# Hybrid encoder step on one core: the mixers' stores and the gate preparation's transfers issued from GpSimd instead of SyncE

## The chip, the cores and the metric

The kernel runs on one core of one Trainium2 chip. The metric is device time in microseconds (us), the median of several executions; less is better. The engines are called TensorE (PE in the profile), VectorE (DVE), ScalarE (ACT), GpSimd (POOL) and SyncE (SP). PE multiplies matrices, DVE, ACT and POOL work on elements, and SP computes nothing: it issues DMA transfers, in the order of its own program. ACT and POOL can issue DMAs too, each in its own order.

## The reference

One layer of an encoder works on two groups that share weights: a prompt of 2048 tokens, and 8 streams with 16 new tokens each. Width 1024, feed-forward 2816.

```python
h = rms_norm(x, norm_g[0])
z = h @ w_in
qa, ka, va, qb, kb, vb, ob, ib, fb = jnp.split(z, IN_SPLITS, axis=-1)
att = band_attention_prompt(...)  # streams: band_attention_step
att = rms_norm(att, g_att)
hb, (c1, n1, m1) = mlstm_sequence(qh, kh, vh, ig, lf, c0, n0, m0)
hb = hb * lax.rsqrt(jnp.mean(hb * hb, axis=-1, keepdims=True) + EPS)
mlstm_out = (hb * g_mlstm * jax.nn.sigmoid(ob)).astype(x.dtype)
mix = jnp.concatenate([att, mlstm_out], axis=-1) @ w_out
x = x + rms_norm(mix, norm_g[1])
ffn, new_buf = conv_ffn(rms_norm(x, norm_g[2]), conv_buf, w_up, w_conv, b_conv, w_down)
x = x + rms_norm(ffn, norm_g[3])
```

The attention has 8 heads of 64, each over its chunk and the 8 chunks before it. The second mixer, an mLSTM, has 4 heads of 128 with a matrix state `c` per head, a normaliser `n` and a running maximum `m`; its gates `ig` and `lf` weigh products of queries and keys by exponentials of cumulative sums. All is float32. The new keys and values, `c`, `n`, `m` and the last rows of the convolution are outputs too.

## The kernel before, in words

The tokens stand in 17 tiles of 128 rows, 16 of the prompt (`SEQ`) and one of the streams (`SAMPLE`). A float32 product is made as three products of two rounded pieces: `mm3` (L95, L96, L97) issues them, so nearly all of PE's rows carry these lines. Casts and subtractions on ACT and DVE make the pieces (`qs`, `kh`, `skh` and so on).

**Stages.** Until about 1066 us the kernel runs through two halves of the tokens with 14 column groups of `w_in` each (names `va`, `qk`, `qb`, `vo`; results `qk_st` and so on are copied out of PE's memory at L224 and L226 and stored by ACT's DMAs at L239). Between these products a planner (`pump`) lays pieces of two streams of work, the attention (`heads`) and the mLSTM (`mems`). Then comes the output projection (`project`, rows of `wo`, until about 1340 us), and then the feed-forward blocks, which the change doesn't touch.

**Data through device memory.** Much is stored to device memory by one step and read back in another layout by a later one:

- `load_head` (L325 to L351) loads `nb` (a band of the relative bias, from `relrow`), `qraw`, `kraw` and `vraw` of an attention head out of `qTd`, `kTd`, `vd`. POOL then clears two corners of `nb` (L326, L327). L440 stores the head pair's result `attst` to `mixd`.
- `prep_sample` (L600 to L626) and `prep_prompt` (L553 to L585) prepare the gates. They store rows `md` and `dd` to device memory, and read `dd` back at once as `dec`, spread over 128 partitions. `mlstm` loads `mb` from `md` (L664), and POOL masks it (L673).
- `finish_heads` (L640 to L655) ends a pair of mLSTM tiles: `ad` and `mf` on POOL, `num` on DVE, then the store of `num` to `mixd` (or `mixs` for the streams).
- `mlstm_sample` goes through the 8 streams' states in four steps `bp` of two: load `cs` (L769), `qz` on POOL (L771, L774), products `cus` on PE (L781, L782), the new `cs` on DVE, its store to `c_sample` (L787). `cs` has two buffers.
- `attention_sample` loads cached keys `skr` and values `svr` of a stream (L847, L897), POOL copies the new columns into `skr` (L848), ACT casts to `skh` (L852), and L911 stores the result to `atts`.
- `project` loads the mixers' rows `mr` back, multiplies, normalises with a root that POOL makes (L78, L84, `n_rs`, `att_rs`), adds the input `xr` on POOL (L1027) and stores the tile to `x2d` (L1028). `mx` and `xr` share one buffer of two, which the load of L1004 fills again.

**What sets the order.** The kernel is built with a scheduler that simulates its own timeline and writes each engine's order from it; buffers come free when their last reader, a DMA included, is done. Each DMA also gets a completion lane. SP and ACT share eight of them in turn, and an issue waits until the transfer that last had its lane has landed; transfers of POOL have eight lanes of their own. An engine that waits, for data, a buffer or a lane, holds all that stands behind it in its order.

Of the kernel before, what the change touches and what calls it, by code (L numbers as in the profile page):

```python
# [17 lines left out]
P = 128  # L18
# [3 lines left out]
DB = 8  # L22
DS = 16
HA = 8
DA = 64
HB = 4
DH = 128
# [17 lines left out]
def hymba_step(ctx: ExitStack, tc: tile.TileContext, I: dict, O: dict):  # L45
    nc = tc.nc
# [317 lines left out]
    def att_unit(s, g2, j):  # L364
# [68 lines left out]
        for jj in range(4):  # L433
# [3 lines left out]
            st.rearrange("p a (h d) -> p a h d", h=2),  # L437
            ao.rearrange("p (a h d) -> p a h d", a=4, h=2),
            rinv.unsqueeze(3).broadcast_to([P, 4, 2, DA]), op=ALU.mult)
        nc.sync.dma_start(mixd[kg][:, :, pair * P:(pair + 1) * P], st)  # L440
        yield 0.43, 0.7

    def att_stream():
# [103 lines left out]
    def prep_prompt(half):  # L547
        n = 8
        ig, lf, nlf = log_gates(1 + 8 * half, n, f"p{half}")
        f2 = lambda t: t.rearrange("p c h -> p (c h)")  # L550
        yield 0.3, 0.8
        a, b = cum_rows(f2(ig), f2(lf), f2(nlf), 32, tri, f"p{half}")
        ca = pm.tile([P, P], F32, tag="kw", name=f"cm{half}", bufs=2)[:32, :]  # L553
        nc.vector.tensor_tensor_scan(ca, a, a, NEG, op0=ALU.max, op1=ALU.max)
        yield 0.3, 0.4
        rt = ps_sm(f"rt{half}")
        transpose(rt[0:1, 0:32], ca[:, P - 1:P], 32)
        transpose(rt[0:1, 32:64], b[:, P - 1:P], 32)
        row = pm.tile([1, 2, n, HB], F32, tag="rowl", name=f"rowl{half}", bufs=1)
        nc.vector.tensor_copy(row.rearrange("p a c h -> p (a c h)"), rt[0:1, 0:64])  # L560
        o = 8 * half
        for h in range(HB):
            nc.vector.tensor_tensor_scan(mrow[:, o + 1:o + 9, h], row[:, 0, :, h], row[:, 1, :, h],
                                         mrow[:, o:o + 1, h], op0=ALU.max, op1=ALU.add)
        yield 0.3, 0.5
        mp = ps_sm(f"mp{half}")
        transpose(mp[0:32, 0:1], mrow[:, o:o + 8, :].rearrange("p c h -> p (c h)"), 1)
        mprev = small.tile([32, 1], F32, tag="mprev", name=f"mprev{half}")
        nc.vector.tensor_copy(mprev, mp[0:32, 0:1])
        yield 0.3, 0.8  # L570
        pk = pm.tile([P, P], F32, tag="kw", name=f"pk{half}", bufs=2)
        nc.vector.tensor_scalar(ca, ca, mprev, None, op0=ALU.max)
        nml = small.tile([32, 1], F32, tag="nml", name=f"nml{half}")
        nc.vector.tensor_scalar(nml, ca[:, P - 1:P], -1.0, None, op0=ALU.mult)
        nc.vector.tensor_copy(pk[0:32, :], a)
        nc.scalar.activation(pk[32:64, :], ca, AF.Exp, bias=mprev, scale=-1.0)
        nc.vector.tensor_tensor(b, b, ca, op=ALU.add)
        nc.scalar.activation(pk[64:96, :], b, AF.Exp, scale=-1.0)
        nc.scalar.activation(pk[96:128, :], a, AF.Exp, bias=nml)
        md = dt_([32, P], f"md{half}")  # L580
        dd = dt_([32, 1], f"dd{half}")
        nc.sync.dma_start(md, ca)
        nc.sync.dma_start(dd, pk[32:64, P - 1:P])
        dec = pm.tile([P, n, HB], F32, tag="dec", name=f"dec{half}", bufs=1)
        nc.sync.dma_start(dec, dd.rearrange("(c h) o -> o c h", c=n).broadcast_to([P, n, HB]))  # L585
        yield 0.0, 0.8
        cols = pack_columns(pk, "p")
        stab[half] = (md, dec, cols)
        yield 0.3, 0.8

    def prep_sample():
        ig, lf, nlf = log_gates(0, 1, "s")
        trib = pm.tile([P, P], F32, tag="wexp", name="trib", bufs=2)
        nc.gpsimd.affine_select(out=trib, in_=tri, pattern=[[-DS, DB], [0, DS]], compare_op=ALU.is_ge, fill=0.0,
                                base=0, channel_multiplier=1)
        reset = pm.tile([P, P], F32, tag="kw", name="reset", bufs=2)[:HB, :]
        nc.gpsimd.memset(reset, 0.0)
        nc.gpsimd.memset(reset.rearrange("p (b s) -> p b s", b=DB)[:, :, 0:1], NEG)
        f2 = lambda t: t.rearrange("p c h -> p (c h)")
        a, b = cum_rows(f2(ig), f2(lf), f2(nlf), HB, trib, "s")  # L600
        yield 0.3, 0.8
        ms = small.tile([HB, DB], F32, tag="mss", name="mss")
        nc.sync.dma_start(ms, I["state_m"])
        ca = pm.tile([P, P], F32, tag="kw", name="cms", bufs=2)[:HB, :]
        nc.vector.tensor_tensor_scan(ca, reset, a, 0.0, op0=ALU.add, op1=ALU.max)
        v3 = lambda t: t.rearrange("p (b s) -> p b s", b=DB)
        msb = ms.unsqueeze(2).broadcast_to([HB, DB, DS])
        nc.vector.tensor_tensor(v3(ca), v3(ca), msb, op=ALU.max)
        mn_ = small.tile([HB, DB], F32, tag="mnew", name="mnew")
        nc.vector.tensor_tensor(mn_, v3(ca)[:, :, DS - 1], v3(b)[:, :, DS - 1], op=ALU.add)  # L610
        nc.sync.dma_start(O["m_sample"], mn_)
        pk = pm.tile([P, P], F32, tag="kw", name="pks", bufs=2)
        nc.vector.memset(pk, 0.0)
        nc.vector.tensor_copy(pk[0:HB, :], a)
        nc.vector.tensor_tensor(v3(pk[32:32 + HB, :]), msb, v3(ca), op=ALU.subtract)
        nc.vector.scalar_tensor_tensor(pk[64:64 + HB, :], b, -1.0, ca, op0=ALU.mult, op1=ALU.subtract)
        nc.vector.tensor_tensor(v3(pk[96:96 + HB, :]), v3(a), v3(ca)[:, :, DS - 1:DS].broadcast_to([HB, DB, DS]),
                                op=ALU.subtract)
        for o in (32, 64, 96):
            nc.scalar.activation(pk[o:o + HB, :], pk[o:o + HB, :], AF.Exp)  # L620
        md = dt_([HB, P], "mds")
        dd = dt_([HB, DB], "dds")
        nc.sync.dma_start(md, ca)
        nc.sync.dma_start(dd, v3(pk[32:32 + HB, :])[:, :, DS - 1])
        dec = pm.tile([P, HB, DB], F32, tag="decs", name="decs", bufs=1)
        nc.sync.dma_start(dec, dd.unsqueeze(0).broadcast_to([P, HB, DB]))  # L626
        yield 0.0, 0.8
        cols = pack_columns(pk, "s")
        stab["s"] = (md, dec, cols)
        yield 0.3, 0.8  # L630


    def finish_heads(num, enm, og, h, nch, dst, name):

        den = num[:, :, 0]
        ad = small.tile([P, 2], F32, tag="ad", name=f"ad{name}")[:, :nch]
        ssq = small.tile([P, 2], F32, tag="mssq", name=f"mssq{name}")[:, :nch]
        nc.vector.scalar_tensor_tensor(ad, den, -1.0, den, op0=ALU.mult, op1=ALU.max)
        nc.vector.tensor_tensor(ad, ad, enm, op=ALU.max)
        for c in range(nch):  # L640
            jk = pm.tile([P, P], F32, tag="wexp", name=f"jk{name}_{c}", bufs=2)
            nc.scalar.activation(jk, num[:, c, 1:DH + 1], AF.Square, accum_out=ssq[:, c:c + 1])
        nc.vector.tensor_tensor(ad, ad, ad, op=ALU.mult)
        nc.vector.scalar_tensor_tensor(ad, ad, DH * EPS, ssq, op0=ALU.mult, op1=ALU.add)
        f = small.tile([P, 2], F32, tag="mf", name=f"mf{name}")[:, :nch]
        nc.gpsimd.tensor_scalar(ad, ad, 1.0 / DH, 0.0, op0=ALU.mult, op1=ALU.add)
        nc.gpsimd.tensor_tensor(f, ad, nhalf[:, :nch], op=ALU.pow)
        nc.scalar.activation(og, og, AF.Tanh, scale=0.5)
        nc.vector.scalar_tensor_tensor(og, og, 1.0,
                                       hgm[h].unsqueeze(1).broadcast_to([P, nch, DH]),  # L650
                                       op0=ALU.add, op1=ALU.mult)
        for c in range(nch):
            nc.vector.scalar_tensor_tensor(num[:, c, 1:DH + 1], num[:, c, 1:DH + 1], f[:, c:c + 1], og[:, c, :],
                                           op0=ALU.mult, op1=ALU.mult)
        nc.sync.dma_start(dst, num[:, :, 1:DH + 1])  # L655

    def mlstm(h, half):
        md, dec, cols = stab[half]
# [21 lines left out]
        def chunk(s, c):  # L680
# [29 lines left out]
            finish_heads(num, cols[:, 2, r0:r0 + HB + 1:HB], s.og, h, 2,  # L710
                         mixd[sg][:, o:o + 2, 512 + h * DH:512 + (h + 1) * DH], s.nm)
            if half == 1 and s.pc == 3:
                nc.sync.dma_start(O["c_prompt"][h], cst[h])
            yield 0.0, 1.3

        pairs = [SimpleNamespace(pc=pc, t0=8 * half + 2 * pc, nm=f"{h}_{8 * half + 2 * pc}") for pc in range(4)]
# [9 lines left out]
    def mlstm_sample(h):  # L726
# [38 lines left out]
        def batches(bp):  # L765
# [18 lines left out]
                                           op0=ALU.mult, op1=ALU.add)  # L784
            nc.vector.tensor_tensor(cs, cs, dec[:, h, bs].unsqueeze(2).broadcast_to([P, 2, e]), op=ALU.mult)
            nc.vector.tensor_tensor(cs, cs, cu[:, :2 * e].rearrange("p (b e) -> p b e", b=2), op=ALU.add)
            nc.sync.dma_start(O["c_sample"][h][:, bs], cs)  # L787
            yield 0.85, 0.8

        def finish():  # L790
# [28 lines left out]
    def attention_sample(b0, b1):  # L819
# [74 lines left out]
        def values(b, kk):  # L894
# [13 lines left out]
            if kk == 4:  # L908
                so = pa.tile([P, 512], F32, tag="attT", name=f"so{b}", bufs=1)
                nc.vector.tensor_scalar(so, s.ot, s.rs, None, op0=ALU.mult)  # L910
                nc.sync.dma_start(atts[b], so)  # L911
            yield 0.64, 0.1

        yield queries()
# [47 lines left out]
    def project(tiles):  # L962
# [34 lines left out]
        for n_, s in enumerate(ss):  # L997
# [27 lines left out]
            rs = rsqrt_mean(ssq, D, f"n1_{t}", ssa)  # L1025
            nc.vector.scalar_tensor_tensor(m, m, rs, g1[0], op0=ALU.mult, op1=ALU.mult)
            nc.gpsimd.tensor_tensor(xr, m, xr, op=ALU.add)  # L1027
            nc.sync.dma_start(x2d[t], xr)  # L1028

# [224 lines left out]
                mems.append(lambda i=i: mlstm_sample(i))  # L1256
    for cost in out:
        pump(*cost)
    nc.sync.dma_start(O["m_prompt"], mrow[:, 16, :])


    p3, halo = ffn.p3, ffn.halo
# [431 lines left out]
```

## Time and profile before

| | |
|---|---|
| median of 3 executions | 2796.95 us (2793.69 to 2801.31) |
| the profiled execution, its own time | 2796.47 us |
| its span in the profile | 2794.8 us |
| mean granted clock of TensorE | 0.996 |
| PE, DVE, ACT, POOL busy | 2729.5, 1877.1, 1407.9, 429.6 us |
| moved to and from device memory | 486.05 MB, 174 GB/s in the mean |

The queues of DMAs in use were SP's, with 274590 packets and 449.21 MB, and ACT's, with 38592 packets and 33.83 MB; two queues of instructions carry the remaining 3 MB. POOL issued none.

Reading the rows: in a table of waits stand the engine and line that waited, what ended the wait, then microseconds in total, how often, and the longest. "SPq" is SP's queue of DMA issues, "ACTq" that of ACT. A timeline row has its start and duration in us, engine, line, operation, output and input, and in brackets the idle time just before it with what ended it. A row by stretch of time has for each engine busy us and the number of instructions, then TensorE's granted clock, the share of the DMA engines that was busy, and GB/s. A group's row ends with shortest, median and longest nanoseconds, or for a DMA with the median us from issue to landing.

### The profile page before, as it was taken

Reading aid. Unit: us, or ns where it says so; the run is one execution under the profiler, and the core shown is the slowest. Engines: PE = TensorE matmul, PEld = TensorE weight load, DVE = VectorE, ACT = ScalarE, POOL = GpSimd, SP = SyncE. Lnnn points to the kernel's source line nnn. Section 1 sums busy time; section 2 is a strip of 40 time slices with the busy share of each in tenths; the row PEclk is TensorE's granted clock in tenths of the full one; section 3 lists DMA queues with packets and bytes.
Section 4 is the critical chain, followed back from the end, with each engine's and each line's share of the span. In section 5 each row is a group of like instructions: output and inputs, shape, how many; then the busy total and the mean of one; then the engine's idle time right before and its main releaser. Section 6 shows DMA issues by size and latency. Waiting matters only on the chain.

```text
span 2794.8 us, 47058 instructions
## 1 busy us (share of the span) xinstructions
PE 2729.5 (98%) x16587; PEld 2554.0 (91%) x16587; DVE 1877.1 (67%) x3442; ACT 1407.9 (50%) x2836; POOL 429.6 (15%) x876
## 2 busy tenths in 40 slices
PE   8899999999999999999999999999999999999998
PEld 7899999998899998888999988899999878999887
DVE  5244455655556668766999986457777864888855
ACT  4354555534356666534545555345455543555543
POOL 1000010211100002344211110011111210222221
PEclk9999999999999999999999999999999999999999
DMA  5534355557555456346655555644444774555685
GB/s 187 150 117 137 105 169 162 164 151 212 160 174 149 140 170 185 114 157 220 199 175 167 169 177 174 220 142 153 160 154 140 275 267 151 172 177 177 195 299 192
DMA packets 313419, 486.05 MB, mean 174 GB/s; under 512 B 55426, under 2 KB 150622, under 8 KB 313054
## 3 DMA queue, kind: packets, MB, share of 16 engines
q1 hardware_dynamic: 274590, 449.21, 50.7%
q10 hardware_dynamic: 38592, 33.83, 3.6%
q8 instruction: 130, 2.13, 0.3%
q14 instruction: 107, 0.88, 0.1%
HBM read 359.36 MB, written 126.70 MB: 174 GB/s over the span
## 4 chain that ended last, share of the span: by engine, by line
PE 55%; DVE 2%; DMA 1%; issue 1%; POOL 1%; ACT 1%; SPq 0%; DVEq 0%; POOLq 0%; ACTq 0%
PE uec L95 6%; PE uec L96 6%; PE uec L97 6%; PE dn L97 4%; PE dn L96 4%; PE dn L95 4%; PE ua L97 3%; PE ua L96 3%; PE ua L95 3%; PE dnm L97 2%; PE dnm L95 2%; PE dnm L96 2%; PE wo L97 2%; PE wo L95 2%; PE wo L96 2%; PE ub L96 1%
## 5 line engine op out<-in xcount | busy, mean ns | idle before, releaser
L95 PE MATMUL uec<-B,wuh 128*128 128x384 f32 (+1 forms) x720 | 234.9, 328 | 0.9 <-DVE uu L1418 0.7
L96 PE MATMUL uec<-B,wuh 128*128 128x384 f32 (+1 forms) x720 | 235.2, 327 | 0.0
L97 PE MATMUL uec<-B,wul 128*128 128x384 f32 (+1 forms) x720 | 234.0, 327 | 0.0
L1266 DVE TENSOR_TENSOR gl<-gr,gh 128x768 fp32r<-128x768 f32 (+3 forms) x141 | 121.7, 872 | 154.1 <-ACT gh L1265 145.7
L1265 ACT CAST gh<-gr 128x768 fp32r<-128x768 f32 (+3 forms) x141 | 102.0, 736 | 200.1 <-PE dn L96 184.3
L1265 ACT CAST wuh<-wu 128x512 fp32r<-128x512 f32 x255 | 141.7, 618 | 113.0 <-PE uec L96 100.9
L95 PE MATMUL dn<-wdh,gh 128*128 128x512 f32 x466 | 182.9, 393 | 2.2 <-DVE ug L1418 2.2
L96 PE MATMUL dn<-wdl,gh 128*128 128x512 f32 x466 | 184.1, 395 | 0.0
L97 PE MATMUL dn<-wdh,gl 128*128 128x512 f32 x466 | 168.3, 396 | 0.0
L1266 DVE TENSOR_TENSOR wul<-wu,wuh 128x512 fp32r<-128x512 f32 x255 | 164.7, 684 | 2.8 <-DMA x2d<-mx 2.8
L393 DVE CUSTOM_DVE_ANT_0 tmp<-s,nb 128x640 f32<-128x640 f32 (+4 forms) x128 | 94.4, 737 | 92.5 <-PE s L383 91.1
L95 PE MATMUL vo<-wi_h,hT 128*128 128x256 f32 x544 | 155.9, 287 | 0.6 <-DVE mt L199 0.6
L97 PE MATMUL vo<-wi_h,hT 128*128 128x256 f32 x544 | 156.4, 288 | 0.0
L96 PE MATMUL vo<-wi_l,hT 128*128 128x256 f32 x544 | 155.6, 286 | 0.0
L95 PE MATMUL qk<-hT,wi_h 128*128 128x384 f32 (+1 forms) x384 | 129.8, 338 | 8.7 <-ACT qk_st L224 7.7
L95 PEld LDWEIGHTS uec<-B,wuh 128*128 128x128 f32 x720 | 135.1, 188 | 2.7 <-DVE uu L1418 1.2
L96 PEld LDWEIGHTS uec<-B,wuh 128*128 128x128 f32 x720 | 135.4, 188 | 0.2
L97 PEld LDWEIGHTS uec<-B,wul 128*128 128x128 f32 x720 | 135.2, 188 | 0.0
L406 DVE TENSOR_TENSOR ptl<-pt,pth 128x640 fp32r<-128x640 f32 (+4 forms) x128 | 93.6, 737 | 54.9 <-ACT pth L405 53.7
L394 ACT ACTIVATE tmp<-tmp,mn 128x640 f32<-128x640 f32 (+4 forms) x128 | 97.6, 762 | 64.5 <-DVE mn L393 62.1
L96 PE MATMUL qk<-hT,wi_h 128*128 128x384 f32 (+1 forms) x384 | 129.1, 336 | 0.0
L97 PE MATMUL qk<-hT,wi_l 128*128 128x384 f32 (+1 forms) x384 | 128.7, 335 | 0.0
(411 smaller groups left out, 8876.7 us busy)
## 6 DMA issues: line engine op xcount, KB each, us to landing
wu<-in_w_up SPq DMA_DIRECT2D x220, 256.0 KB, 4.0
wu<-wsd SPq DMA_DIRECT2D x176, 256.0 KB, 4.8
wdr<-in_w_down SPq DMA_DIRECT2D x132, 256.0 KB, 5.1
gr<-gd SPq DMA_DIRECT2D x78, 384.0 KB, 4.2
wi_raw<-in_w_in SPq DMA_DIRECT2D x52, 512.0 KB, 3.9
wsd<-ws SPq DMA_DIRECT2D x88, 256.0 KB, 2.7
gd<-g SPq DMA_DIRECT2D x44, 384.0 KB, 3.5
kraw<-kTd SPq DMA_DIRECT2D x112, 128.0 KB, 3.4
```

What stands on the lines that cost most here:

```text
L95: nc.tensor.matmul(out, ah, bh, start=start, stop=False, skip_group_check=onto)
L96: nc.tensor.matmul(out, ah, bl, start=False, stop=False, skip_group_check=onto)
L97: nc.tensor.matmul(out, al, bh, start=False, stop=stop, skip_group_check=onto)
L393: nc.vector.tensor_tensor_reduce(o_, s_, b_, 1.0, 3e38, ALU.add, ALU.min, accum_out=mn)
L394: nc.scalar.activation(tmp[:, :n], tmp[:, :n], AF.Exp, bias=mn, scale=-1.0, accum_out=rsum[:, i % 4, hh:hh + 1])
L406: nc.vector.tensor_tensor(s.ptl[:, sl, qc], ptv, s.pth[:, sl, qc], op=ALU.subtract)
L1265: nc.scalar.copy(h, r)
L1266: nc.vector.tensor_tensor(l, r, h, op=ALU.subtract)
```

## The change

At 15 places the call of a DMA moves from SP to POOL. In all 109 transfers move. Data, sizes and destinations stay as they are.

```diff
-        nc.sync.dma_start(mixd[kg][:, :, pair * P:(pair + 1) * P], st)
+        nc.gpsimd.dma_start(mixd[kg][:, :, pair * P:(pair + 1) * P], st)
...
-        nc.sync.dma_start(md, ca)
-        nc.sync.dma_start(dd, pk[32:64, P - 1:P])
+        nc.gpsimd.dma_start(md, ca)
+        nc.gpsimd.dma_start(dd, pk[32:64, P - 1:P])
         dec = pm.tile([P, n, HB], F32, tag="dec", name=f"dec{half}", bufs=1)
-        nc.sync.dma_start(dec, dd.rearrange("(c h) o -> o c h", c=n).broadcast_to([P, n, HB]))
+        nc.gpsimd.dma_start(dec, dd.rearrange("(c h) o -> o c h", c=n).broadcast_to([P, n, HB]))
...
-        nc.sync.dma_start(dst, num[:, :, 1:DH + 1])
+        nc.gpsimd.dma_start(dst, num[:, :, 1:DH + 1])
...
-            nc.sync.dma_start(O["c_sample"][h][:, bs], cs)
+            nc.gpsimd.dma_start(O["c_sample"][h][:, bs], cs)
...
-                nc.sync.dma_start(atts[b], so)
+                nc.gpsimd.dma_start(atts[b], so)
...
-            nc.sync.dma_start(x2d[t], xr)
+            nc.gpsimd.dma_start(x2d[t], xr)
```

These are L440 (16 transfers), L582, L583 and L585 (two each), L655 (36), L787 (16), L911 (8) and L1028 (17). The same is done with the load of `ms` (L603), the stores of `m_sample` (L611), `mds` and `dds` (L623, L624), the load of `decs` (L626), the four stores of `c_prompt` (L713) and that of `m_prompt` (L1259). Further back, in the feed-forward blocks, SP goes on issuing stores too (`wsd`, `gd`, `f0d`, the outputs).

Since the scheduler orders every engine anew, rows move that the diff doesn't name. ACT in the first column group, where `qk_st` of the first `qk` group is copied out and `qs` of the first attention head is cast from the loaded `qraw`:

```order
 L224 COPY qk_0_st_0_1068<-qk_0_1_0_1000 128x384
 L239 DMA kTd_0_78<-qk_0_st_0_1068 128x384
-L342 CAST qs_0_1290<-qraw_0_1263 128x512
 L224 COPY qk_0_st_1_1110<-qk_0_1_1_1071 128x384
 L239 DMA kTd_0_78<-qk_0_st_1_1110 128x128
 L239 DMA kTd_1_79<-qk_0_st_1_1110 128x256
+L342 CAST qs_0_1290<-qraw_0_1263 128x512
 L1175 CAST wi_h_1165<-wi_raw_1180 128x512 x2
```

The cast now comes behind the copy of `qk_st` and its stores. SP a little later in the same stretch, from the load of a `w_in` piece on, where `prep_prompt` had its transfers:

```order
 L1169 DMA wi_raw_1245<-in_w_in 128x1024
 L337 DMA kraw_0_0_1335<-kTd_0_78 64x512 x2
-L582 DMA md_1136<-cm_1065 32x128
-L583 DMA dd_1137<-pk_1127 32x1
 L351 DMA vraw_0_0_1367<-vd_0_114 128x4x64
-L585 DMA dec_1140<-dd_1137 128x32
-L302 DMA relrow<-ext 128x767 x2
+L334 DMA qraw_1_1484<-qTd_1_95 64x512 x2
 L1169 DMA wi_raw_1446<-in_w_in 128x1024
-L334 DMA qraw_1_1484<-qTd_1_95 64x512 x2
```

`md`, `dd` and `dec` are gone from SP, and the last two broadcasts of `relrow` (which now stand ahead of the first `qraw`) no longer precede the `wi_raw` load. The third place is the second half's `prep_prompt`, beside the cached keys of stream 6. On SP before:

```order
L847 DMA skr6_0_9190<-in_cache_k 128x512
L847 DMA skr6_1_9219<-in_cache_k 128x512
L582 DMA md1_8472<-cm1_8367 32x128
L583 DMA dd1_8473<-pk1_8463 32x1
L664 DMA mb0_8_10342<-md1_8472 128x2x128
L585 DMA dec1_8476<-dd1_8473 128x32
L847 DMA skr6_2_9248<-in_cache_k 128x512
L847 DMA skr6_3_9280<-in_cache_k 128x512
```

On POOL now, while SP issues the four `skr6` loads in a row:

```order
L848 COPY skr6_0_9190<-own4_8631 128x16
L848 COPY skr6_1_9219<-own4_8631 128x16
L582 DMA md1_8472<-cm1_8367 32x128
L848 COPY skr6_2_9248<-own4_8631 128x16
L583 DMA dd1_8473<-pk1_8463 32x1
L848 COPY skr6_3_9280<-own4_8631 128x16
L585 DMA dec1_8476<-dd1_8473 128x32
L673 AFFINE_SELECT mb0_8_10342<-mb0_8_10342 128x256
```

The preparation's three transfers have changed queue: they stood between two pairs of loads, and stand now between POOL's copies into the same buffers.

More of the change, by code (lines that the diff above doesn't have):

```diff
@@ L602, in prep_sample @@
         ms = small.tile([HB, DB], F32, tag="mss", name="mss")
-        nc.sync.dma_start(ms, I["state_m"])
+        nc.gpsimd.dma_start(ms, I["state_m"])
         ca = pm.tile([P, P], F32, tag="kw", name="cms", bufs=2)[:HB, :]
@@ L610, in prep_sample @@
         nc.vector.tensor_tensor(mn_, v3(ca)[:, :, DS - 1], v3(b)[:, :, DS - 1], op=ALU.add)
-        nc.sync.dma_start(O["m_sample"], mn_)
+        nc.gpsimd.dma_start(O["m_sample"], mn_)
         pk = pm.tile([P, P], F32, tag="kw", name="pks", bufs=2)
@@ L622, in prep_sample @@
         dd = dt_([HB, DB], "dds")
-        nc.sync.dma_start(md, ca)
-        nc.sync.dma_start(dd, v3(pk[32:32 + HB, :])[:, :, DS - 1])
+        nc.gpsimd.dma_start(md, ca)
+        nc.gpsimd.dma_start(dd, v3(pk[32:32 + HB, :])[:, :, DS - 1])
         dec = pm.tile([P, HB, DB], F32, tag="decs", name="decs", bufs=1)
-        nc.sync.dma_start(dec, dd.unsqueeze(0).broadcast_to([P, HB, DB]))
+        nc.gpsimd.dma_start(dec, dd.unsqueeze(0).broadcast_to([P, HB, DB]))
         yield 0.0, 0.8
@@ L712, in chunk @@
             if half == 1 and s.pc == 3:
-                nc.sync.dma_start(O["c_prompt"][h], cst[h])
+                nc.gpsimd.dma_start(O["c_prompt"][h], cst[h])
             yield 0.0, 1.3
@@ L1258, in hymba_step @@
         pump(*cost)
-    nc.sync.dma_start(O["m_prompt"], mrow[:, 16, :])
+    nc.gpsimd.dma_start(O["m_prompt"], mrow[:, 16, :])
     p3, halo = ffn.p3, ffn.halo
```

## The prediction

> **What bounds the kernel now.** First the page's busy shares, then busy time by stage (the mixers and the projection end at about 1340 us; behind that come the feed-forward blocks, whose instruction order the change leaves as it was).
>
> ```profile
> PE 2729.5 (98%) x16587; PEld 2554.0 (91%) x16587; DVE 1877.1 (67%) x3442; ACT 1407.9 (50%) x2836; POOL 429.6 (15%) x876
> ...
> 0.00:60.00 60.00, 46.54 (x335) 44.82 (x336) 33.63 (x66) 28.77 (x50) 9.61 (x33) 1.00 0.52 173
> 60.00:440.00 380.00, 370.32 (x2579) 362.90 (x2579) 175.89 (x429) 182.03 (x430) 12.16 (x45) 0.99 0.48 141
> 440.00:760.00 320.00, 304.85 (x2134) 290.65 (x2133) 180.78 (x496) 151.25 (x381) 51.86 (x152) 0.99 0.56 168
> 760.00:1066.00 306.00, 304.42 (x2311) 299.01 (x2310) 190.28 (x435) 190.68 (x457) 19.08 (x61) 0.99 0.55 163
> 1066.00:1340.00 274.00, 268.15 (x1439) 226.57 (x1437) 197.76 (x293) 134.48 (x308) 102.94 (x134) 1.00 0.53 173
> ```
>
> TensorE is the bound: in the 2794.8 us of the span it works 2729.5. A change of DMA queues cannot shorten its work; it can only close or open gaps. Between 60 and 1340 us, where moved transfers stand, the gaps are 380 − 370.3 = 9.7, then 15.2, 1.6 and 5.9, together 32.3 us. That, and stretches at a low granted clock, is all that can be won. The list of waits says what ends the gaps before a late matmul.
>
> ```profile
> PE qk L95 <- ACT qk_st L224: 7.7, 2, 4.4
> PE cus L781 <- DMA cs<-in_state_c: 5.6, 6, 1.9
> PE ss L95 <- ACT skh L852: 3.4, 3, 2.8
> SPq L1028 <- POOL mx L1027: 84.9, 14, 17.8
> SPq L655 <- DVE num L653: 42.9, 15, 11.8
> SPq L440 <- DVE attst L436: 40.4, 10, 8.9
> SPq L1004 <- DMA x2d<-mx: 26.3, 11, 4.4
> SPq L769 <- DMA out_c_sample<-cs: 24.6, 7, 4.4
> ```
>
> SP stands 84.9 + 42.9 + 40.4 us in front of stores whose data isn't made. Yet almost no gap of TensorE is put down to a load that such a wait held: the loads were issued early enough. Hence this large figure is not the gain.
>
> **Part 1, the gaps that the move can close.** The first two, in the instruction rows of ACT, SP and PE:
>
> ```profile
> 68.94 0.33 ACTq L239 DMA_DIRECT2D qTd<-qk_st  x1
> 81.71 0.62 ACT L342 CAST qs<-qraw 128x512 fp32r<-128x512 f32 x1 [10.93 <-DMA qraw<-qTd]
> 82.24 0.47 ACT L224 COPY qk_st<-qk 128x384 f32<-128x384 f32 x1
> 82.76 0.44 PE L95 MATMUL qk<-hT,wi_h 128*128 128x384 f32 x1 [3.23 <-ACT qk_st L224]
> 97.57 0.34 SPq L585 DMA_DIRECT2D dec<-dd  x1
> 98.36 1.17 SPq L302 DMA_DIRECT2D relrow<-ext  x2
> 99.64 0.52 SPq L1169 DMA_DIRECT2D wi_raw<-in_w_in  x1
> 108.18 0.81 ACTq L239 DMA_DIRECT2D qTd<-qk_st  x2
> 109.64 0.69 PE L95 MATMUL qk<-hT,wi_h 128*128 128x384 f32 x1 [4.43 <-ACT qk_st L224]
> 110.00:115.00 5.00, 5.00 (x18) 5.00 (x18) 0.60 (x3) 1.53 (x5) 0.82 (x2) 0.50 0.53 148
> ```
>
> At 82.76 TensorE waits 3.23 us because ACT, in order, stands behind the cast of `qs`, which waits for its load. In the new order the evacuation comes ahead of that cast: 3.2 us won, and I count it whole. At 109.64 ACT had stood before its store of `qTd`, which shares, by the order, a completion lane with the `wi_raw` load of 99.64; that load follows two broadcasts of `relrow`, and these stand behind `dec`. The new order has the broadcasts some 30 us earlier and no `dec` on SP. The gap of 4.43 was followed by 5 us at clock 0.50, which cost 2.5: 6.9 us. Lanes are dealt anew, so another store can meet another load; I count half, 3.5. The third is at 745:
>
> ```profile
> 732.38 1.31 SPq L583 DMA_DIRECT2D dd<-pk  x1
> 738.85 0.34 SPq L585 DMA_DIRECT2D dec<-dd  x1
> 739.28 0.86 SPq L847 DMA_DIRECT2D skr<-in_cache_k  x2
> 744.60 0.63 ACT L852 CAST skh<-skr 128x528 fp32r<-128x528 f32 x1 [9.14 <-DMA skr<-in_cache_k]
> 745.00:750.00 5.00, 4.71 (x21) 4.71 (x22) 3.02 (x5) 2.96 (x7) 0.41 (x1) 0.66 0.53 157
> ```
>
> `dec` reads back what `dd` stored and waits for its landing; two `skr` loads stand behind it, ACT waits for them 9.14 us, TensorE 2.77 (2.8 is the longest in the row on `skh`), then 5 us at 0.66 lose 1.7: 4.5 us. The new order has four `skr` loads in a row. But their own columns are copied by POOL, which now issues `md`, `dd` and `dec` between those copies, and the casts wait for the copies. Half again: 2.2. Gains: 3.2 + 3.5 + 2.2 = 8.9.
>
> **Part 2, the price of a store from POOL.** The trace has no DMA of POOL's; its price is bounded by rows. The low end is what SP pays (0.34 to issue, 4.6 to land for the state below), and no less, since the same 16 DMA engines carry it. For the high end stand the longest of POOL's operations, and a row on VectorE: 128x512 by a scalar takes 478 ns at least but mostly 2606, as long as POOL's 2392 ns addition that runs beside it. One engine evidently waits out the other.
>
> ```profile
> L1027 POOL TENSOR_TENSOR mx<-mx x17: 2370/2392/2798, 1079.0 to 1329.5; 128x1024 f32<-128x1024 f32 x17
> L985 DVE TENSOR_SCALAR mr<-mr,att_rs x17: 478/2606/2623, 1014.6 to 1304.4; 128x512 f32<-128x512 f32 x17
> L84 POOL TENSOR_TENSOR n_rs<-n_ms,nhalf x56: 537/548/567, 5.7 to 2788.5; 128x1 f32<-128x1 f32 x56
> out_c_sample<-cs SPq DMA_DIRECT2D x16, 129.0 KB, 4.6
> ```
>
> So the extra between "data ready" and "landed" lies between 0 and 2.4 us. A POOL operation on one element takes 0.55, so I don't believe the low end, and the wait on a busy neighbour isn't met by every store, so not the high one: the middle, 1.2.
>
> The Trainium skill (DMA: Bandwidth & Descriptors, Latency and other measured facts) gives a transfer issued by GpSimd, whose own cores write its descriptors, some 1 us to the first byte, and one by SP or ACT 0.6. By that the extra would be an estimated 0.4, and part 2 a third of what follows; no run here shows it yet. The same page (Issuing engines are not separate DMA queues) says that spreading issues saves only the sequencer's issue time, which speaks against any large gain.
>
> **Where that extra is on the path.** The state of the sample heads has two buffers: a store must land before SP loads the next state into it.
>
> ```profile
> 566.66 0.34 SPq L787 DMA_DIRECT2D out_c_sample<-cs  x1
> 571.30 0.33 SPq L769 DMA_DIRECT2D cs<-in_state_c  x1
> 573.61 0.68 PE L781 MATMUL cus<-cs,qz 128*128 128x129 f32 x4 [0.37 <-DMA cs<-in_state_c]
> ```
>
> Store 566.66, landed and reloaded 571.30, needed 573.61, TensorE already late by 0.37. Four heads have two such reuses each, and 6 of the 8 are in the list of waits, with 5.6 us. The new order has much the same matmuls between them, so the extra comes on top: 8 × 1.2 = 9.6; ends 0 and 8 × 2.4 = 19. Behind the last of these stores POOL makes `ads` and `mfs` of that head, which VectorE needs for `nums`: a few us of VectorE time, with TensorE on other work, counted 1 (0 to 4 × 1.2 = 5 if that cover is gone).
>
> In the projection POOL issues `x2d` behind its own addition and ahead of the next tile's root, for which VectorE waits already.
>
> ```profile
> DVE mx L1026 <- POOL n_rs L84: 14.0, 14, 1.9
> ACT mx L1016 <- POOL mx L1027: 42.3, 8, 6.1
> ```
>
> 17 stores × 1.2 are 20 us more on POOL, whose 102.94 of 274 us leave room; VectorE has 274 − 197.8 = 76 us free there. I count a fifth, 4 us; ends 0 and, with 2.4 and half passed on, 20. `attst`, `num`, `atts`, `c_prompt` and `m_prompt` are read much later or never; TensorE's work on other heads hides their landing, so nothing (without that cover, 1.2 each). The late loads that SP no longer holds only come sooner into buffers that were in time. The other gaps, 32.3 − (3.2 + 4.4 + 2.8 + 5.6) = 16.3 us, are dealt anew by the new order: 0, ends −8 and +8.
>
> **Sum.** −8.9 + 9.6 + 1 + 4 = +5.7 on the profiled 2796.47 us, which is 1.7 above its span and 0.5 below the median of 2796.95: 2802 to 2803. I say **2803**, its own range 2794 to 2812.
>
> **Rivals.** (a) *All three gaps close and POOL's price is nil*: −3.2 − 6.9 − 4.5 = −14.6, so 2782. For it speak the new rows on ACT and SP; against it the lanes, and that `skr` now depends on POOL twice. (b) *VectorE starves POOL's stores.* At 2.4 a store the reuses cost 19, `ads` 1 and the projection 10; the longest gaps (1.9 + 2.4 = 4.3) are then near the 4.43 that was followed by clock 0.50, 2.5 more for perhaps three. Less the gains of 8.9 that is +29, so 2825 at the far end, and 2817 with half of the projection's and the clock's terms. It decides from an extra of about 1.6 us on (8 × 1.6 + 5 − 8.9 = 8.9). For it speak the 2606 ns row and a VectorE busy for 180.78 of 320 us in the sample stage; against it, POOL's root never takes over 567 ns in 56 rows.
>
> The Trainium skill (SBUF — State Buffer, SBUF: two separate sides, and the section behind it) names this: a GpSimd DMA's descriptors can't be written while VectorE runs a two-port operation, and 620 ns become 3100; that would be an estimated 2.5 a store. Row L985 agrees that the two engines wait for each other; no run here shows it for a DMA.
>
> (c) *The change doesn't do what it says*: SP's waits only change name, since the loads at L1004, L769 and L664 must now await the landing of POOL's stores, and hold SP as before; POOL in turn waits for SP's loads.
>
> ```profile
> POOL nb L326 <- DMA nb<-relrow: 397.3, 14, 79.9
> POOL mb L673 <- DMA mb<-md: 148.7, 23, 39.1
> ```
>
> A store queued behind such a wait is late by it. If this eats the gains, 3.2 stays won against half of the losses, 14.6 / 2 − 3.2 = +4: 2801.
>
> **How the numbers follow.** 0.3%, some 8.4 us, is about what a measurement tells from no change: faster is under 2788.5, slower above 2805. Forecast 0.42 (0.19 of it above 2805, where its own range ends), (a) 0.30, (b) 0.22, (c) 0.06. Faster 0.30; same 0.23 + 0.06 = 0.29; slower 0.19 + 0.22 = 0.41. The range takes in most of (a) and (b): 2778 to 2825.
>
> **What would show it.** Part 1: no wait of `qk` for `qk_st` near 80 to 110 us, and no `skh` wait of 2.8. Part 2: the wait of `cus` for `cs`, 5.6 us before, grows to about 15; at 6 the price was nil, at 25 it is (b). Landing times of the moved stores, POOL's rows, and VectorE's wait at L1026 tell the extra directly. The forecast falls if gaps of TensorE appear at other places, as the new order could make.

## The result and the profile after

The changed kernel takes 2804.28 us (median of 20 runs, 2798.47 to 2809.16), the kernel before 2794.34 in 20 runs beside it. The ratio is 1.0037, with a 95% interval of 1.0031 to 1.0044: slower by some 10 us. The forecast was 2803, or +6 on its profiled execution. The number held; most of the reasons behind it did not, as the experiments show. One of the prediction's own signs says the same: gaps of TensorE appeared at other places.

The page of the changed kernel, with its busy shares and the queues of SP and POOL, then its list of TensorE's waits:

```profile
PE 2731.2 (97%) x16587; PEld 2554.1 (91%) x16587; DVE 1871.6 (67%) x3442; ACT 1405.7 (50%) x2836; POOL 507.8 (18%) x985
...
q1 hardware_dynamic: 249696, 427.08, 48.4%
...
q0 software_dynamic: 7312, 22.13, 2.2%
```

```profile
PE cus L781 <- DMA cs<-in_state_c: 10.5, 7, 3.5
...
PE qk L95 <- ACT qk_st L226: 5.4, 1, 5.4
PE ma L698 <- DVE num L704: 3.6, 2, 2.0
...
PE pkTs L67 <- ACT pks L620: 3.2, 1, 3.2
...
PE ss L95 <- ACT skh L852: 1.4, 2, 0.9
```

TensorE works as much as before (2731.2 us against 2729.5) in a span of 2802.2 against 2794.8. The difference is mostly gaps. The wait for `skh` is down from 3.4 to 1.4 us; the early wait for `qk_st`, which was to go, is 5.4; `cus` waits 10.5 in place of 5.6; `ma`, 0.5 before, waits 3.6, and `pkTs` is new. The 109 transfers are on POOL's queue now, and POOL is 78 us busier.

Where the 7.4 us of span came from shows when the n-th matmul of the one trace is set against the n-th of the other (their start times from the span's start; the order differs, so this is good to about a microsecond):

| time before, us | 54 | 117 | 453 | 622 | 716 | 812 | 1042 | 1322 | 2697 |
|---|---|---|---|---|---|---|---|---|---|
| later after the change, us | 0.3 | 2.4 | 6.8 | 3.0 | 9.2 | 4.1 | 5.7 | 5.2 | 6.6 |

So 2.4 us are lost at the start and 4.4 between 117 and 453; then 3.8 are won up to 622, some 6 lost in the sample stage near 700, and 5 won between 716 and 812, where the `skh` gap and the low clock behind it had been. Up to 1042 another 1.6 are lost. The projection from there on costs nothing (VectorE waits 14.5 us for POOL's root at L1026, 14.0 before), and what lies behind it adds 2 us.

**The start.** Rows of ACT and TensorE in the changed kernel:

```profile
71.45 3.28 ACTq L239 DMA_DIRECT2D qTd<-qk_st  x2
74.78 0.97 ACT L620 ACTIVATE pks<-pks 4x128 f32<-4x128 f32 x3 [9.41 <-DMA relrow<-ext]
75.80 0.36 PE L67 MATMUL pkTs<-ident,pks 128*128 128x128 f32 x1 [3.25 <-ACT pks L620]
106.26 0.69 ACT L689 ACTIVATE w<-mb,colsp 128x128 f32<-128x128 f32 x2 [8.82 <-POOL mb L673]
107.38 0.69 PE L95 MATMUL qk<-hT,wi_h 128*128 128x384 f32 x1 [5.37 <-ACT qk_st L226]
```

The cast of `qs` no longer precedes the copy of `qk_st`, as the order had shown, and the 3.23 us at 82.76 are gone. But the `relrow` broadcasts, no longer held by the preparation on SP, are issued earlier, and ACT's store of `qTd` waits for one of them. `pks` stands behind the store, and TensorE waits 3.25 us at another place. The second gap also has a new reason: the scheduler put ACT's `w`, which needs POOL's mask of `mb`, ahead of the copy of `qk_st`. Both gaps were closed and both were opened again.

**411 us.** VectorE and TensorE in the changed kernel:

```profile
410.67 0.23 DVE L492 TENSOR_SCALAR hgms<-hgms 128x128 f32<-128x128 f32 x1 [3.08 <-DMA hgms<-in_g_mlstm]
...
411.15 0.49 PE L698 MATMUL ma<-cst,mqk 128*128 128x129 f32 x2 [2.05 <-DVE num L704]
```

The order now puts `hgms`, whose load from SP is late, ahead of the `num` that TensorE needs. No moved transfer is in this chain; only the order is new.

**SP's waits**, which the title of the change is about:

```profile
SPq L1004 <- DMA x2d<-mx: 63.5, 10, 20.2
...
SPq L978 <- DVE mr L985: 35.9, 6, 8.9
...
SPq L671 <- DVE num L653: 34.7, 17, 10.4
...
SPq L769 <- DMA mixd<-num: 21.5, 7, 6.0
SPq L769 <- DMA out_c_sample<-cs: 19.7, 6, 5.5
```

The 84.9, 42.9 and 40.4 us at the stores are gone from the list. In their place the loads wait for the very things that the stores had waited for: L671 for `num`, 34.7 us, and L1004 for the landing of `x2d`, 63.5 in place of 26.3. Such waits now stand on POOL as well, the longest before the stores of `attst`:

```profile
POOL mixd L440 <- DVE attst L436: 236.7, 10, 55.7
```

POOL's masks and copies for TensorE stand in the same order behind such a store. What this costs TensorE is not shown.

### The profile page after: what moved, and what is told of

Its sections match the earlier page's. It is cut to its first block, busy times and chain, and to the rows that moved or that the text cites. A ratio compares the mean times of both kernels' runs of the same rounds, so it can differ in the third digit from the quotient of the medians.

```text
span 2802.2 us, 47164 instructions
## 1 busy us (share of the span) xinstructions
PE 2731.2 (97%) x16587; PEld 2554.1 (91%) x16587; DVE 1871.6 (67%) x3442; ACT 1405.7 (50%) x2836; POOL 507.8 (18%) x985
## 3 DMA queue, kind: packets, MB, share of 16 engines
q1 hardware_dynamic: 249696, 427.08, 48.4%
q0 software_dynamic: 7312, 22.13, 2.2%
q8 instruction: 130, 2.13, 0.3%
## 4 chain that ended last, share of the span: by engine, by line
PE 67%; DMA 7%; DVE 5%; issue 2%; ACT 2%; POOL 1%; ACTq 0%; SPq 0%; DVEq 0%; POOLq 0%
PE uec L95 5%; PE uec L96 5%; PE uec L97 5%; PE dn L97 4%; PE dn L96 4%; PE dn L95 4%; PE ua L97 3%; PE ua L96 3%; PE ua L95 3%; PE dnm L97 2%; PE dnm L95 2%; PE dnm L96 2%; PE wo L97 2%; PE wo L95 2%; PE wo L96 2%
```

## The experiments

All times are medians. Each ratio is to runs of the kernel before on the same chip, with its interval; it is not the quotient of two medians. For att_only the two differ most: 1.0014 is some 4 us, while its median is 7.3 us above that of the kernel before beside it, 2796.80.

| run | what differs from before | time, us | ratio, 95% interval |
|---|---|---|---|
| cs_only | L787 on POOL | 2795.38 | 0.9997, 0.9988 to 1.0006 |
| prep_relrow | preparation and `relrow` on POOL | 2796.41 | 1.0000, 0.9986 to 1.0014 |
| num3 | third buffer for `num` and `cs` | 2796.76 | 1.0004, 0.9995 to 1.0013 |
| prep_only | preparation on POOL | 2798.76 | 1.0010, 1.0001 to 1.0019 |
| att_only | L440, L911 on POOL | 2804.11 | 1.0014, 1.0003 to 1.0026 |
| mix_only | L440, L655, L911 on POOL | 2805.79 | 1.0032, 1.0020 to 1.0045 |
| the change | all 15 calls | 2804.28 | 1.0037, 1.0031 to 1.0044 |
| redeal | no transfer moves | 2809.10 | 1.0039, 1.0025 to 1.0052 |
| redeal2 | no transfer moves | 2810.94 | 1.0048, 1.0034 to 1.0062 |
| all_but_num | the change without L655 | 2815.00 | 1.0059, 1.0045 to 1.0072 |
| num_only | L655 on POOL | 2818.40 | 1.0079, 1.0059 to 1.0099 |
| plain_before | scheduler without its timeline | 2904.73 | 1.0387, 1.0368 to 1.0405 |
| plain_after | the change, scheduler without its timeline | 2908.40 | 1.0397, 1.0379 to 1.0415 |

### One part alone

**prep_only** has the diff's lines L582 to L585 and L603 to L626 alone, **prep_relrow** also this:

```diff
-                tc.keep_in_program_order(nc.sync.dma_start(relrow[h], ext[h:h + 1, :].broadcast_to([P, SQ])))
+                tc.keep_in_program_order(nc.gpsimd.dma_start(relrow[h], ext[h:h + 1, :].broadcast_to([P, SQ])))
```

> Only the gate preparation's transfers (L582 to L585, L603 to L626) go to POOL. Theory from the trace of the change: the gap at 745 (2.8 us and 1.7 us of low clock) goes, as in the changed kernel; the two early gaps stay or move, since the relrow broadcasts, issued earlier, hold ACT's stores of qTd by their completion lanes: TensorE idle 3 us near 76 and 5 us near 107, 2.4 us worse than before. Net about -2.5 us against before. The prediction's own theory: all or most of 3.2 + 6.9 + 4.5 is won, net -9 to -14. Cus waits for cs stay at 5 to 6 us in both.

> As prep_only, and the eight relrow broadcasts on POOL too, whose lanes ACT's stores don't share. Theory 'shared lane': ACT's store of qTd no longer waits near 71 us for a broadcast, both early gaps (3.2 and 5.4 us with 1.7 and about 3 us of low clock) shrink to under 2 us together, net -9 to -13 us against before. Rival 'the DMA engines are full then, whatever the lane': gaps of 3 and 5 us remain, net as prep_only within 2 us.

TensorE's rows with a gap between 75 and 113 us, in prep_only and then in prep_relrow:

```profile
75.32 0.33 PE L67 MATMUL pkTs<-ident,pks 128*128 128x128 f32 x1 [2.12 <-ACT pks L620]
107.25 0.69 PE L95 MATMUL qk<-hT,wi_h 128*128 128x384 f32 x1 [5.66 <-ACT qk_st L226]
```

```profile
91.50 0.44 PE L95 MATMUL qk<-hT,wi_h 128*128 128x384 f32 x1 [2.82 <-ACT qk_st L226]
100.15 0.45 PE L95 MATMUL qk<-hT,wi_h 128*128 128x384 f32 x1 [2.44 <-ACT qk_st L226]
112.76 0.69 PE L95 MATMUL qk<-hT,wi_h 128*128 128x384 f32 x1 [3.95 <-ACT qk_st L224]
```

prep_only has the early gaps of the changed kernel, so the preparation's move, with the new order that comes with it, makes them; the gains of 9 to 14 us that the prediction's theory had for it fall. The gap of `skh` at 745 stayed there too, as 1.9 us at 752, against my expectation, and the kernel is 0.10% slower where 2.5 us less had been expected. In prep_relrow the gap at 76 is gone, as the theory of the shared lane has it. But three others with 9.2 us stand in place of two with 7.8, and the time is that of before: the 9 to 13 us that this theory promised did not come. (The profiled execution of prep_relrow, 2805.02 us, is the slowest of its twelve, so its gaps are rather large.) In the four traces, before and the change included, this stretch loses 7.7 to 9.2 us in such gaps, whichever wait is taken away.

**cs_only** is L787 alone, **mix_only** L440, L655 and L911.

> Only the store of c_sample (L787) goes to POOL. Prediction's theory, 1.2 us more per store: cus waits for cs grow from 5.6 to about 15 us, total +8 to +10 us. Theory from the trace of the change (data ready to reload 4.2 us before, 4.3 after): cus waits 5 to 8 us, total within 3 us of before.

> Only attst, num (nums) and atts (L440, L655, L911) go to POOL. Theory from the trace of the change: the store of num has the price, 2.3 us from data to freed buffer before and 3.7 after; it delays the first two loads of cs of each head, cus waits for cs 8 to 11 us, of which 3 us or more before the first two groups of a head; total +3 to +6 us. Prediction's theory: these stores cost nothing, cus waits 5 to 6 us, total within 3 us of before but for the reordering.

TensorE's waits for the states in cs_only, then in mix_only:

```profile
PE cus L781 <- DMA cs<-in_state_c: 5.9, 5, 2.4
```

```profile
PE cus L781 <- DMA cs<-in_state_c: 8.3, 5, 2.5
```

The stores of `c_sample`, for which the prediction had counted 9.6 us, cost nothing that can be told: 5.9 us of waits, as before, and a ratio of 0.9997. mix_only loses nearly as much as the whole change, some 9 us where 3 to 6 had been expected, and its waits grow, as the theory of the trace had it. This looked like the answer. It is not, as the next runs show.

### The price of num, or the new order

Each edit makes the scheduler deal the work anew. **num_only** and **att_only** split mix_only, **all_but_num** leaves L655 on SP, and **redeal** moves no transfer; it only changes a cost that the planner reads, so that the planner lays the pieces in another order:

```diff
         nc.sync.dma_start(mixd[kg][:, :, pair * P:(pair + 1) * P], st)
-        yield 0.43, 0.7
+        yield 0.43, 0.9
```

> Only the store of num and nums (L655) goes to POOL. Theory 'price of num': it has nearly the whole loss of mix_only (9 us), cus waits for cs 8 to 11 us, total +5 to +9 us. Rival 'order': what costs is that the scheduler deals the work anew, whichever store moves; then num_only and the two kernels att_only and redeal lie at about the same +3 to +9 us.

> Only attst and atts (L440, L911) go to POOL. Theory 'price of num': nobody waits for these stores, total within 3 us of before. Rival 'order': +3 to +9 us.

> No transfer moves; the planner's cost behind the store of attst is 0.9 us in place of 0.7, so that the work is dealt anew about as much as in the change. Theory 'price of num': total within 4 us of before, to either side. Rival 'order': +3 to +9 us.

> The change without L655: num and nums stay on SP. Theory 'price of num': 5 to 8 us less than the changed kernel, so +2 to +5 us against before, cus waits 5 to 7 us. Rival 'order': +6 to +10 us as the changed kernel, or any other value, without regard to num.

**redeal2** has 0.5 there.

> No transfer moves; the planner's cost behind the store of attst is 0.5 us in place of 0.7, a larger new deal than in redeal. Theory 'order': again 3 to 16 us slower than before. If redeal was one bad draw: within 4 us of before.

As the account of the whole loss, the theory of a price of `num` falls. att_only, for whose stores by that theory nobody waits, is 0.14% slower, some 4 us, a little over what that theory allowed. all_but_num, freed of that price, is slower than the change, not faster. num_only is slowest of all, and its waits of `cus` are not up:

```profile
PE cus L781 <- DMA cs<-in_state_c: 5.4, 4, 3.9
```

And redeal and redeal2, in which every transfer stays on its queue, lose 0.39% and 0.48%, as much as the change. The parts do not add up either: num_only and all_but_num together hold all the moves, and lose 1.38% where the change loses 0.37%. The theory of the order had its size wrong too: it gave 3 to 9 us, where redeal lost 11 and num_only 22.

The next table sets the time beside two things. One is how far TensorE's order moved: the rows of a trace in order of their start, by line, operation and names without buffer numbers, are compared with those of before, and rows that went out and rows that came in are added up. The other is TensorE's idle time in the profiled execution, a stretch less its busy time.

| run | rows by which TensorE's order differs, of 16,587 | gaps of 1 us or more before the feed-forward blocks | idle from 60 to 760, and to 1340 us | ratio |
|---|---|---|---|---|
| before | 0 | 9, 19.4 us | 24.8, 7.4 us | 1 |
| prep_only | 260 | 12, 24.4 us | 27.4, 7.0 us | 1.0010 |
| prep_relrow | 286 | 13, 26.4 us | 29.1, 7.8 us | 1.0000 |
| cs_only | 304 | 10, 18.1 us | 22.2, 8.8 us | 0.9997 |
| num3 (no transfer moves) | 388 | 12, 22.6 us | 25.5, 7.0 us | 1.0004 |
| redeal (no transfer moves) | 746 | 14, 24.9 us | 22.9, 13.8 us | 1.0039 |
| att_only | 924 | 12, 24.5 us | 28.8, 6.2 us | 1.0014 |
| redeal2 (no transfer moves) | 1020 | 14, 25.7 us | 23.4, 14.4 us | 1.0048 |
| mix_only | 1234 | 14, 24.9 us | 25.0, 10.1 us | 1.0032 |
| all_but_num | 1734 | 13, 26.9 us | 30.8, 8.8 us | 1.0059 |
| num_only | 2268 | 17, 32.8 us | 30.0, 14.6 us | 1.0079 |
| the change | 2296 | 14, 28.5 us | 28.7, 7.6 us | 1.0037 |

(The gaps are counted from the starts and ends of TensorE's rows up to the first `uec`.) The four orders that differ by up to 388 rows lie within 0.10% of before; the seven that differ by more lose 0.14 to 0.79%. Among the seven, the time doesn't follow the distance. The redeals are also smaller deals than the change, a third and less than half of its rows, and not about as much, as had been expected. (The larger counts in the expectations, 619 and 824 lines, are of another kind of comparison, which counts neighbouring lines too.)

Where the time goes differs as well. The views by windows of before, of the change, of redeal and of redeal2, in that order:

```profile
60.00:760.00 700.00, 675.18 (x4711) 653.55 (x4711) 356.66 (x924) 333.27 (x811) 64.01 (x197) 0.99 0.51 154
760.00:1340.00 580.00, 572.57 (x3748) 525.59 (x3746) 388.04 (x727) 325.16 (x765) 122.02 (x195) 1.00 0.54 168
...
60.00:760.00 700.00, 671.28 (x4689) 650.61 (x4688) 354.35 (x921) 329.54 (x806) 104.16 (x258) 0.99 0.51 153
760.00:1340.00 580.00, 572.44 (x3748) 524.46 (x3747) 381.08 (x727) 323.03 (x766) 155.41 (x241) 1.00 0.53 166
...
60.00:760.00 700.00, 677.08 (x4736) 655.52 (x4735) 359.54 (x927) 335.13 (x816) 65.51 (x199) 1.00 0.52 155
760.00:1340.00 580.00, 566.18 (x3685) 517.35 (x3683) 374.34 (x716) 316.29 (x753) 120.99 (x193) 0.99 0.52 162
...
60.00:760.00 700.00, 676.58 (x4731) 654.51 (x4730) 358.48 (x928) 333.82 (x815) 64.70 (x199) 1.00 0.52 154
760.00:1340.00 580.00, 565.65 (x3690) 517.02 (x3689) 375.61 (x718) 315.47 (x753) 120.48 (x192) 0.99 0.52 163
```

Up to 760 us, where the change idles 3.9 us longer than before, the two redeals idle less than before; they lose behind 760, where the change loses nothing. So they show that a new order alone can cost 0.4 to 0.5%, and not that it is what cost the change. In the first stretch the four kernels with every transfer on SP idle 22.9 to 25.5 us, and six of the eight with moved transfers 27.4 to 30.8; cs_only and mix_only, with 22.2 and 25.0, do not fit. With one profile of each, that points back to the moved transfers without deciding it.

### The order nearly held

To see the queues apart from the order, both kernels were built with the scheduler's timeline off. Between these two, TensorE's order differs by 308 rows only, counted as in the table; that is a seventh of the 2296.

```diff
-    with tile.TileContext(nc, schedule_with_timeline_sim=True) as tc:
+    with tile.TileContext(nc, schedule_with_timeline_sim=False) as tc:
```

> The kernel before, but the scheduler runs without its own timeline, so that the order follows the program far more closely. Its time itself tells nothing; it is the partner of plain_after. Probably some per cent slower than before.

> The changed kernel, with the scheduler run without its timeline: against plain_before the change moves about a ninth as many of TensorE's rows as it does with the timeline, so that what the queues cost is seen with the order nearly held. Theory 'order': within 4 us of plain_before, to either side. Theory 'price of POOL's stores': 7 to 15 us slower than plain_before.

The pair stands at 1.0387 and 1.0397 of before: a difference of 0.10%, some 3 us (3.7 by the medians), with intervals of 0.2% to each side on either, so that zero isn't excluded, nor some 10 us. That fits the theory of the order and leaves the lower part of the other theory's 7 to 15 us open. In the profiled executions the feed-forward blocks begin at 1397.9 and 1398.4 us. The price of one store can be read here, since the same reuse stands in both. The first reuse of a state buffer, in plain_before and in plain_after:

```profile
404.78 0.41 DVE L786 TENSOR_TENSOR cs<-cs,cus 128x258 f32<-128x258 f32 x1
405.22 0.35 SPq L787 DMA_DIRECT2D out_c_sample<-cs  x1
407.02 0.34 SPq L769 DMA_DIRECT2D cs<-in_state_c  x1
```

```profile
401.42 0.41 DVE L786 TENSOR_TENSOR cs<-cs,cus 128x258 f32<-128x258 f32 x1
402.13 0.58 POOL L787 DMA_DIRECT2D out_c_sample<-cs  x1 [0.69 <-DVE cs L786]
...
404.35 0.34 SPq L769 DMA_DIRECT2D cs<-in_state_c  x1
```

From VectorE's end to the reload it is 1.8 us over SP and 2.5 over POOL; over the eight reuses 2.13 and 2.72, or 0.6 more. For `num`, from VectorE's end to landing, the trace of plain_before has six of the 32 stores, with a mean of 2.47; the same six take 4.54 in plain_after (all 32 there: 3.87), or 2.1 more. These are real prices, but here TensorE hardly waits for them: `cus` waits 0.7 us in plain_after.

```profile
PE cus L781 <- DMA cs<-in_state_c: 0.7, 3, 0.3
```

The pair has more room for such waits: TensorE idles 75.4 us between 60 and 1340 us in plain_before, and 32.3 in the kernel before. So it bounds the price in this order, and the tighter order of the change may pay more.

### A version without the wait

**num3** is the kernel before, all on SP, with a third buffer:

```diff
-                s.num = pm.tile([P, 2, e], F32, tag="num", name=f"num{s.nm}", bufs=2)
+                s.num = pm.tile([P, 2, e], F32, tag="num", name=f"num{s.nm}", bufs=3)
...
-            cs = pm.tile([P, 2, e], F32, tag="num", name=f"cs{h}_{bp}", bufs=2)
+            cs = pm.tile([P, 2, e], F32, tag="num", name=f"cs{h}_{bp}", bufs=3)
```

> The kernel before, all stores on SP, with three buffers in place of two for num and cs, so that a load of cs waits for an older store; the order changes at few rows (824 lines of difference on TensorE, 619 in cs_only). If the waits of cus for cs (5.6 us) are on the path and the new deal is small: cus waits under 2 us, total -3 to -6 us, faster than before and than the change. If the new deal decides even here: anything from -3 to +4.

The list of TensorE's waits has no line for `cs` any more, and in its upper part:

```profile
PE qk L95 <- ACT qk_st L224: 6.3, 2, 3.4
PE ss L95 <- ACT skh L852: 5.6, 4, 2.2
...
PE ms L686 <- DMA mqk<-qkbd: 2.2, 1, 2.2
```

The 5.6 us are gone and the time is the same: `ss` waits 5.6 in place of 3.4, and 2.2 us for `mqk` stand where there were 0.7. Here a gap that was closed came back somewhere else.

## Why the prediction was right, and where it was not

**Direction and size: right, 2803 against 2804.28.** That the sum came so near is luck: its terms erred to both sides, by up to some 9 us, and the errors cancelled.

**Part 1, the early gaps (−6.7 counted): failed.** The order was read rightly for the row of `qs`, but what the freed `relrow` broadcasts would meet was only priced as a half chance. They met ACT's store of `qTd`, and the stretch lost 2.4 us instead. **The gap at 745 (−2.2 counted, half of 4.5): right, and whole**, 4 to 5 us in the changed kernel. The preparation alone doesn't close it (1.9 us in prep_only), which suggests that this too belongs to the particular order.

**Part 2, the price of a store from POOL (1.2 chosen between 0 and 2.4): right in the mean and not for either store**: 0.6 for `c_sample`, the store that the sum used it for, and 2.1 for `num`, counted as nothing, with the order nearly held. In the traces of before and of the change the four `num` stores that can be compared take 3.23 and 5.40, or 2.2 more. The Trainium skill's first-byte figures (DMA: Bandwidth & Descriptors, Latency and other measured facts) had given an estimated 0.4; the measured prices are above it.

**Where that price is on the path (9.6 + 1 + 4 counted): failed.** cs_only shows 0 in place of 9.6 (from 3 us less to 2 us more by its interval). The changed kernel's `cus` waits did grow by 4.9, to less than the 15 foretold. Over the eight reuses of its state buffers, data to reload takes 4.19 us before and 4.30 after, so hardly any of that growth is the store of `c_sample`. Most of it is at the first two loads of a head, which wait for `num`: their gaps are 5.2 us after and 1.4 before. The prediction had put all six waits before down to the reuses; two of them, these 1.4 us, belonged to `num`, whose store it counted as nothing. Yet num3 shows that these waits can vanish without a gain, so no price is to be set on them one by one. The projection's 4 us are 0.

**The new order (0 counted, −8 to +8): the least founded step.** It was put down as noise around zero for 16 us of other gaps. Two kernels with nothing but a new order lose 0.39% and 0.48%, 11 and 13 us, which is outside that range. What was missed is that none of the eleven other deals tried here is faster than the old order, with its 9 gaps of a microsecond or more, beyond its interval, so that a new deal isn't even-handed. Why the old one is so good stays open.

**Rivals.** (a), all gaps close, is out: other gaps opened. (b), VectorE starves POOL's stores, is not seen: POOL's issues of a kind all take nearly the same time, though VectorE is busy for 735 of the 1280 us between 60 and 1340, as the rows of the changed kernel by line show (shortest, median, longest ns):

```profile
L440 POOL DMA_DIRECT2D mixd<-attst x16: 709/731/767, 160.9 to 1214.4; - x16
L655 POOL DMA_DIRECT2D mixd<-num x32: 737/790/811, 388.3 to 1183.6; - x32
L787 POOL DMA_DIRECT2D out_c_sample<-cs x16: 540/541/587, 453.0 to 730.2; - x16
L1028 POOL DMA_DIRECT2D x2d<-mx x17: 575/633/652, 1086.0 to 1340.0; - x17
```

The five-fold stretching of which the Trainium skill warns (SBUF — State Buffer, SBUF: two separate sides, and the section behind it) does not occur in these 81. From issue to landing the longest of a kind takes up to 3.3 times the shortest (L655, 1.9 to 6.3 us), not far from what seven stores of `x2d` did over SP (2.6 to 7.6). Smaller delays behind the issue aren't excluded by this: the 2.1 us of `num` lie above the 1.6 from which on (b) was to decide. (c) came true in part: SP waits 986 us between 60 and 1340 us where it waited 940 before (all its waits in that stretch, added up), under other names. That agrees with the Trainium skill (DMA: Bandwidth & Descriptors, Issuing engines are not separate DMA queues), by which there was only issue time to save.

What stays open is how the 10 us of the change divide between the new order and POOL's price. The plain pair puts the price at 3 us with some 7 to either side, in an order with more room. The redeals show that an order alone can cost as much as the change does, but they lose it in another stretch. For two of the change's gaps, at 107 and at 411 us, the rows name the order; for the one at 76 they name the broadcasts that the move set free, and for the first two state loads of a head the landing of `num`. So both have a part, and neither is shown to be the larger.

## What to carry to other kernels

Where a scheduler deals out the work, an edit of a queue is two edits, and the second, a new order, can cost as much as both together: here the change costs 0.37%, and a new order with no transfer moved 0.4 to 0.5%. Run such an empty deal of like size beside the change before a mechanism is credited, compare the two stage by stage and not only in total, and hold the order where that can be had. In a kernel at 98% of its bounding engine, take the order before as one that may be hard to match, and look at what a freed load runs into, not only at what it leaves.

## What the runs showed of the hardware

POOL is occupied by the issue of a store for 0.54 us (129 KB of state) or 0.79 us (`num`), where SP took 0.34 and 0.38, and it begins the state's store 0.30 us after VectorE's last row where SP began after 0.03 (medians of 16 each). The same 22.13 MB that left SP's queue were 24,894 packets there (274,590 − 249,696) and are 7312 on POOL's. The landing itself is not longer in every case. From issue to landing, `c_sample` takes 2.4 us in the median in plain_before (three landings on record) and in plain_after (16), while `num` with `nums` takes 2.3 (eight landings) and 3.6 (36). The 4.6 us over SP that the prediction started from is a single landing.
